# Rotating a matrix on one core: loads and stores in turn on two DMA queues instead of one queue for each direction

## The chip, the core and the metric

The kernel runs on one core of a Trainium2 chip. The core has five instruction streams: TensorE (PE), VectorE (DVE), ScalarE (ACT), GpSimd (POOL) and SyncE (SP). Data moves between the chip's main memory (HBM) and the core's on-chip memory (SBUF) by 16 DMA engines. In this kernel two streams issue DMAs: SyncE, whose DMAs appear in the profile as queue q1, and ScalarE, whose DMAs appear as queue q10. The metric is the time of one execution on the device in microseconds (us); lower is better.

## The reference

```python
def setup_inputs():
    return {
        "x": np.random.randn(8192, 8192).astype(np.float32),
        "k": 1,
    }

def reference(x: np.ndarray, k: int) -> np.ndarray:
    return np.rot90(x, k)
```

With k = 1 the matrix is turned by 90 degrees against the clock: row i of the output is column 8191 - i of the input. It is a transpose with the columns taken from the last to the first. Nothing is added or multiplied. 268 MB are read and 268 MB are written.

## The kernel before, in words

**Tiles.** The input is cut into 16 macro tiles of 1024 rows by 4096 columns (`R`, `W`; KK = 16). A macro tile kk is read by 8 loads (t = 0 to 7) of 128 full rows of the macro tile each, 2 MB per load, and written by 8 stores (j = 0 to 7) of 512 output rows by 1024 columns each, 2 MB per store. Loads are numbered m = 8 kk + t from 0 to 127, outputs n = 8 kk + j from 0 to 127. In the last macro tile two of the outputs are shaped otherwise (`END`).

**Memory.** There are five 2 MB buffers, `LAND` = 2 for loads and `OUTS` = 3 for outputs, and a `ring` that holds one macro tile less one chunk. The first loads also use the output buffers. From load 9 on the loads take the two landing buffers in turn, and output n uses the buffer that output n-3 had, up to the last macro tile. So load n+9 needs what load n+7 brought to be out of the buffer.

**Steps.** For each load m VectorE waits until it has landed, and writes it to the ring with its columns reversed (line 349). Chunks whose output goes through TensorE are only copied; the others are also transposed within 32 x 32 blocks (STREAM_TRANSPOSE). The ring places that load m takes are those that output m-8 gives free, so VectorE first waits until output m-8 has been taken from the ring. An output is made in one of two ways:

- *Moved outputs.* The 32 x 32 blocks are already turned, and have only to be put in their places. This is done by 16 copies of 32 partitions: VectorE does 1 (line 331), GpSimd 9 (line 310), ScalarE 6 (lines 410 and 419). GpSimd waits for ScalarE's share before its eighth piece and for VectorE's before its ninth, so the end of GpSimd's ninth piece says that the whole output is ready (`s_pool`).
- *TensorE outputs.* TensorE transposes 128 x 128 blocks into PSUM (line 387), and ScalarE copies them to the output buffer (line 429). These are j = 0 and 4 in most macro tiles (`BY_PE`), all j in the first and the last one, and j = 0, 2, 4, 6, 7 in the last but one.

So there are 81 moved outputs: j = 1, 2, 3, 5, 6, 7 in 13 macro tiles and j = 1, 3, 5 in one more.

**What sets the order.** Each engine runs its own list of instructions in the order in which it was written, and waits on semaphores in between: `by_gpsimd`, `by_sync`, `by_vector`, `by_tensor`, `by_scalar`. There is no scheduler. A wait ahead of a DMA therefore holds all that comes behind it in the list of the engine that issues the DMA. `taken(wait, m)` waits until load m has been reversed out of its buffer, `room_for(wait, n)` until the buffer of output n is free, `load_in_turn(e, m)` waits for the buffer's last load to be taken and issues load m.

**Queues.** The first ten loads (`EARLY`) are spread over both queues: 0, 2 and 4 on SyncE, 1, 3 and 5 on ScalarE, and 6 to 9 in halves on both (`BOTH`). From load 10 on, all loads are issued by SyncE (`by_sync`, line 313), and all 128 stores by ScalarE (line 437), each at the end of ScalarE's own work for that output: for a moved output after a wait for `s_pool`, for a TensorE output after its copies out of PSUM.

Of the kernel before, what the change touches and what calls it, by code (L numbers as in the profile page):

```python
# [6 lines left out]
P = 128  # L7
# [10 lines left out]
CH = G * P  # L18
# [6 lines left out]
BY_PE = [0, 4]  # L25
EARLY = range(T + 2)
BOTH = EARLY[-4:]

END = T // 2

# [31 lines left out]
def kernel(tc: tile.TileContext, x: bass.AP, k: bass.AP, out: bass.AP):  # L62
    nc = tc.nc
# [3 lines left out]
    N, M = x.shape  # L67
    dt = x.dtype
    macros = [(r0, c0) for r0 in range(0, N, R) for c0 in range(0, M, W)]
    KK = len(macros)  # L70
    n_out = KK * J
    n_load = KK * T
# [3 lines left out]
    outs = [(kk, range(T), [j]) for kk in range(KK - 1) for j in range(J)]  # L76
# [5 lines left out]
    outs = [(*o, [(j, g * P) for j in reversed(o[2]) for g in range(G)]) for o in outs]  # L82
# [6 lines left out]
    def in_quadrants(kk, j):  # L89
        return j not in by_pe(kk)  # L90

    moved = [in_quadrants(kk, js[0]) for kk, _, js, _ in outs]
# [3 lines left out]
    for n, (kk, ts, js, blocks) in enumerate(outs):  # L96
        if moved[n]:
            continue
        rows = len(ts) * P
# [14 lines left out]
    def moved_until(n):  # L114
        return sum(moved[: n + 1])

    def turned_until(n):
        return sum(len(parts[i]) for i in range(n + 1) if i in parts)

    with tc.tile_critical():  # L120
        head = nc.alloc_sbuf_tensor("head", [P, HEAD], dt)
        ident, scratch = head[:, :P], head[:, P : P + 1]
        bufs = [nc.alloc_sbuf_tensor(f"buf{i}", [P, F], dt) for i in range(LAND + OUTS)]
# [11 lines left out]
        s_store = [nc.alloc_semaphore(f"s_store{i}") for i in range(LAND + OUTS)]  # L135
        s_rev = nc.alloc_semaphore("s_rev")
        s_half = nc.alloc_semaphore("s_half")
        s_ev = nc.alloc_semaphore("s_ev")
# [4 lines left out]
        s_pool = nc.alloc_semaphore("s_pool")  # L143

        def load_buf(m):
            if m < T:
                return m % (LAND + OUTS)
            return LAND + 2 if m == T else (m - T - 1) % LAND

        def out_buf(n):  # L150
            e = n - (KK * J - J)
            if e < 0:
                return LAND + (n + 1) % OUTS
            ends = [load_buf(n_load - 2)]
            ends += [LAND + (KK * J - J + i + 1) % OUTS for i in range(OUTS)]
            ends += [load_buf(n_load - 1)]
            return ends[e % len(ends)]

        def once(e):
            seen = {}  # L160

            def wait(sem, n):
                if seen.get(sem, 0) < n:
                    seen[sem] = n
                    e.wait_ge(sem, n)

            return wait

        def room_for(wait, n):
            b = out_buf(n)  # L170
            stores = [i for i in range(n) if out_buf(i) == b]
            loads = [i for i in range(n_load) if load_buf(i) == b]
            if stores:
                wait(s_store[b], 16 * len(stores))
            elif loads:
                taken(wait, loads[-1])

        def taken(wait, m):
            kk, t = divmod(m, T)
            wait(s_rev, max(rev[m, j] for j in range(J)))  # L180
            if t == T - 1 and kk < KK - 1:
                wait(s_corner, kk + 1)  # L182
# [18 lines left out]
        for m in range(n_load):  # L201
            kk, t = divmod(m, T)
# [16 lines left out]
        def at(v, first, dims):  # L219
            return bass.AP(  # L220
                tensor=v.tensor, offset=v[:, first : first + 1].offset, ap=[v.ap[0], *dims]
            )
# [11 lines left out]
        def moves(n, share):  # L234
            kk, ts, (j,), _ = outs[n]
            rows = len(ts) * P
            places = [slot(kk, t, j) for t in ts if (t, j) != (T - 1, J - 1)]
            ((step, tiles),) = strides(places, CH)
            for a, q in share:
                yield (  # L240
                    at(
                        bufs[out_buf(n)][q * Q : q * Q + Q, :],
                        a * Q,
                        [[rows, G], [P, tiles], [1, Q]],
                    ),
                    at(
                        ring[a * Q : a * Q + Q, :],
                        places[0] * CH + q * Q,
                        [[P, G], [step, tiles], [1, Q]],
                    ),  # L250
                )
# [3 lines left out]
        def load(e, m):  # L255
            r0, c0 = macros[m // T]
            b = load_buf(m)
            rows = slice(0, P)
            if m in BOTH:
                rows = slice(0 if e is nc.sync else 1, P, 2)  # L260
            r = r0 + m % T * P
            e.dma_start(  # L262
                out=bufs[b][rows, :], in_=x[r : r + P, c0 : c0 + W][rows, :]
            ).then_inc(s_land[b], 16)

        def queues(m):
            if m in BOTH:
                return [nc.sync, nc.scalar]
            return [nc.scalar if m in EARLY and m % 2 else nc.sync]

        def load_in_turn(e, m):
            if e not in queues(m):
                return
            last = [i for i in range(m) if load_buf(i) == load_buf(m)]
            taken(e.wait_ge, last[-1])
            load(e, m)

        def landings(m):
            return 16 * sum(1 + (i in BOTH) for i in range(m + 1) if load_buf(i) == load_buf(m))

# [4 lines left out]
        for m in range(LAND + OUTS):  # L285
            for e in queues(m):
                load(e, m)

        def by_gpsimd(e):
# [12 lines left out]
            for n, (kk, _, js, _) in enumerate(outs):  # L302
                if moved[n]:
# [6 lines left out]
                        i = e.tensor_copy(out=to, in_=of)  # L310
                    i.then_inc(s_pool, 1)

        def by_sync(e):
            for m in range(LAND + OUTS, n_load):
                load_in_turn(e, m)
            for b in range(LAND + OUTS):
                n = sum(out_buf(i) == b for i in range(n_out))
                if n:
                    e.wait_ge(s_store[b], 16 * n)
# [76 lines left out]
        def by_scalar(e):  # L396
            wait = once(e)
            e.wait_ge(s_id, 2)
            e.copy(scratch, ident[:, :1])  # L399
            for m in EARLY[LAND + OUTS :]:  # L400
                load_in_turn(e, m)
            for n, (kk, ts, js, blocks) in enumerate(outs):
                r0, c0 = macros[kk]
                rows = len(ts) * P
                b = out_buf(n)
                if moved[n] or (kk < KK - 1 and js[0] == J - 1):
                    room_for(wait, n)
                todo = list(moves(n, pairs[BY_DVE + BY_POOL :])) if moved[n] else []
                for to, of in todo[:1]:
                    e.copy(to, of)  # L410
                if kk < KK - 1 and js[0] == J - 1:
                    e.wait_ge(s_corner, kk + 1)
                    e.copy(  # L413
                        at(bufs[b][:], rows - P, [[rows, G], [1, P]]),
                        at(corner, 0, [[P, G], [1, P]]),
                    ).then_inc(s_freed, 1)
                if moved[n]:
                    for to, of in todo[1:]:
                        i = e.copy(to, of)  # L419
                    i.then_inc(s_act, 1)  # L420
                    e.wait_ge(s_pool, moved_until(n))
                else:
                    for k, h, cols in parts[n]:
                        e.wait_ge(s_half, k + 1)
                        run, deep = len(cols) * P, 1
                        if cols[-1] - cols[0] >= run:
                            run = P * sum(f // rows == cols[0] // rows for f in cols)
                            deep = len(cols) * P // run
                        e.copy(  # L429
                            at(bufs[b][:], cols[0], [[rows, deep], [1, run]]),  # L430
                            at(ps[h][:], 0, [[run, deep], [1, run]]),
                        ).then_inc(s_ev, 1)
                    e.wait_ge(s_ev, turned_until(n))
                groups = len(blocks)
                top = M - c0 - js[0] * CH - groups * P
                left = r0 + ts[0] * P
                e.dma_start(  # L437
                    out=out[top : top + groups * P, left : left + rows].rearrange(
                        "(g m) f -> m g f", m=P
                    ),  # L440
                    in_=bufs[b][:, : groups * rows].rearrange("m (g f) -> m g f", f=rows),
                ).then_inc(s_store[b], 16)

        by_gpsimd(nc.gpsimd)
        by_sync(nc.sync)
        by_vector(nc.vector)
        by_tensor(nc.tensor)
        by_scalar(nc.scalar)


# [33 lines left out]
```

## Time and profile before

| | |
|---|---|
| time, median of 3 runs | 1260.06 us (1260.0 to 1260.36) |
| the profiled execution's own time | 1260.13 us |
| its span | 1258.3 us |
| busy: PE, DVE, ACT, POOL | 332.2, 616.5, 682.0, 803.8 us |
| moved by DMA | 537.22 MB, 427 GB/s over the span |
| queue q10 (ScalarE) | 278.93 MB |
| queue q1 (SyncE) | 257.96 MB |
| last load seen by VectorE | 1209.66 us |
| last store issued | 1243.46 us |

The profile is of one execution. The span is the time from its first to its last instruction. Busy time counts an engine's computing instructions, and not the issue of DMAs nor waits. Of a wait the profile names what ended it. A DMA is shown twice: as an instruction on the engine that issues it (ACTq, SPq), which is done after some hundred nanoseconds, and as bytes moved by the 16 DMA engines. "To landing" is the time from the issue to the completion of the transfer, and holds what the transfer waits in its queue.

### The profile page before, as it was taken

Reading aid. Unit: us, or ns where it says so; the run is one execution under the profiler, and the core shown is the slowest. Engines: PE = TensorE matmul, PEld = TensorE weight load, DVE = VectorE, ACT = ScalarE, POOL = GpSimd, SP = SyncE. Lnnn points to the kernel's source line nnn. Section 1 sums busy time; section 2 is a strip of 40 time slices with the busy share of each in tenths; the row PEclk is TensorE's granted clock in tenths of the full one; section 3 lists DMA queues with packets and bytes.
Section 4 is the critical chain, followed back from the end, with each engine's and each line's share of the span. In section 5 each row is a group of like instructions: output and inputs, shape, how many; then the busy total and the mean of one; then the engine's idle time right before and its main releaser. Section 6 shows DMA issues by size and latency. Waiting matters only on the chain.

```text
span 1258.3 us, 5393 instructions
## 1 busy us (share of the span) xinstructions
PE 332.2 (26%) x1556; PEld 270.3 (21%) x1556; DVE 616.5 (49%) x373; ACT 682.0 (54%) x636; POOL 803.8 (64%) x735
## 2 busy tenths in 40 slices
PE   1556122221112221232202222022220222214474
PEld 0445111211112110121201212012110121203363
DVE  2544554555555555555555555555545554453310
ACT  0334565565556655565556655566555655556454
POOL 0001886767867779676787767877678776795500
PEclk9976555655555555555555555556555565556587
DMA  9999999999999999999999999999999999999998
GB/s 399 418 432 429 429 429 429 431 429 430 428 430 430 430 429 428 431 428 431 429 429 431 428 429 429 431 429 431 428 429 429 430 430 429 429 430 429 430 423 377
DMA packets 36957, 537.22 MB, mean 427 GB/s; under 512 B 4160, under 2 KB 4160, under 8 KB 4160
## 3 DMA queue, kind: packets, MB, share of 16 engines
q10 hardware_dynamic: 19184, 278.93, 52.2%
q1 hardware_dynamic: 17744, 257.96, 48.0%
q8 instruction: 12, 0.20, 0.1%
q14 instruction: 17, 0.14, 0.0%
HBM read 268.44 MB, written 268.44 MB: 427 GB/s over the span
## 4 chain that ended last, share of the span: by engine, by line
DMA 71%; DVE 16%; POOL 5%; ACT 3%; issue 3%; PE 1%; ACTq 0%; SPq 0%; DVEq 0%
DMA buf<-in_x_dram 65%; DVE ring L349 16%; DMA out_dram<-buf 5%; POOL buf L310 5%; ACT buf L429 3%; PE ps L387 1%; ACTq L437 0%; DVE buf L331 0%; PE ps L373 0%; SPq L262 0%; DVE buf L344 0%; DVEq L336 0%; SPq L479 0%; SPq L182 0%; SPq L120 0%
## 5 line engine op out<-in xcount | busy, mean ns | idle before, releaser
L310 POOL COPY buf<-ring 32x1024 f32<-32x1024 f32 (+1 forms) x729 | 803.1, 1102 | 383.9 <-DMA out_dram<-buf 343.6
L387 PE MATMUL ps<-head,ring 128*128 128x128 f32 x1496 | 318.6, 386 | 878.7 <-DVE ring L349 431.5
L387 PEld LDWEIGHTS ps<-head,ring 128*128 128x128 f32 x1496 | 259.6, 201 | 934.9 <-DVE ring L349 440.3
L349 DVE COPY ring<-buf 128x1024 f32<-128x1024 f32 (+5 forms) x152 | 161.6, 1069 | 595.8 <-DMA buf<-in_x_dram 573.6
L419 ACT COPY buf<-ring 32x1024 f32<-32x1024 f32 (+1 forms) x405 | 414.8, 1024 | 4.9
L349 DVE STREAM_TRANSPOSE ring<-buf 128x3072 f32<-128x3072 f32 (+2 forms) x125 | 357.8, 2871 | 0.0
L429 ACT COPY buf<-ps 128x2048 f32<-128x2048 f32 (+1 forms) x133 | 174.2, 1364 | 256.7 <-PE ps L387 182.2
L410 ACT COPY buf<-ring 32x1024 f32<-32x1024 f32 x81 | 82.9, 1023 | 289.9 <-POOL buf L310 230.6
L331 DVE COPY buf<-ring 32x1024 f32<-32x1024 f32 x81 | 108.4, 1339 | 0.0
L373 PE MATMUL ps<-head,buf 128*128 128x128 f32 x60 | 16.7, 434 | 30.3 <-DVE buf L344 30.3
L373 PEld LDWEIGHTS ps<-head,buf 128*128 128x128 f32 x60 | 10.9, 218 | 35.7 <-DVE buf L344 35.7
L413 ACT COPY buf<-ps 128x512 f32<-128x512 f32 x15 | 8.8, 586 | 8.1 <-DMA out_dram<-buf 7.9
L344 DVE COPY buf<-buf 128x512 f32<-128x512 f32 x15 | 5.8, 387 | 0.0
L399 ACT ACT_TABLE_LOAD x1 | 1.3, 1283 | 1.9 <-issue 1.9
L290 POOL MEMSET head<- 128x128 f32 x1 | 0.2, 205 | 0.5 <-SPq L120 0.5
L292 POOL TENSOR_SCALAR_AFFINE_SELECT head<-head 128x128 f32<-128x128 f32 x1 | 0.3, 294 | 0.2 <-POOL head L290 0.2
L465 POOL MEMSET const-float32-0.0<- 128x1 f32 x1 | 0.1, 98 | 0.2 <-issue 0.2
L399 ACT COPY head<-head 128x1 f32<-128x1 f32 x1 | 0.2, 192 | 0.0
L465 POOL MEMSET const-bfloat16-1.0<- 128x1 bf16 x1 | 0.1, 102 | 0.0
L465 POOL MEMSET const-uint8-127<- 128x1 uint8 x1 | 0.1, 101 | 0.0
L465 POOL MEMSET const-float32-1.0<- 128x1 f32 x1 | 0.1, 98 | 0.0
## 6 DMA issues: line engine op xcount, KB each, us to landing
out_dram<-buf ACTq DMA_DIRECT2D x128, 2048.0 KB, 18.5
buf<-in_x_dram SPq DMA_DIRECT2D x121, 2048.0 KB, 15.2
buf<-in_x_dram ACTq DMA_DIRECT2D x3, 2048.0 KB, 17.3
buf<-in_x_dram SPq DMA_DIRECT2D x4, 1024.0 KB, 16.2
buf<-in_x_dram ACTq DMA_DIRECT2D x4, 1024.0 KB, 16.5
```

The source lines that it names most:

```text
L310: i = e.tensor_copy(out=to, in_=of)
L331: i = e.tensor_copy(out=to, in_=of)
L344: e.tensor_copy(out=at(bufs[b][:], 0, [[CH, 1], [1, CH]]), in_=landed(b, js)).then_inc(s_rev, 1)
L349: turn(out=chunk(kk, t, js), in_=landed(b, js)).then_inc(s_rev, 1)
L373: i = e.transpose(corner[:, g * P : g * P + P], bufs[load_buf(m)][:, g * P : g * P + P], ident,)
L387: i = e.transpose(ps[h][:, to : to + P], chunk(kk, t, [j])[:, 0, off : off + P], ident,)
L399: e.copy(scratch, ident[:, :1])
L410: e.copy(to, of)
L413: e.copy(at(bufs[b][:], rows - P, [[rows, G], [1, P]]), at(corner, 0, [[P, G], [1, P]]),).then_inc(s_freed, 1)
L419: i = e.copy(to, of)
L429: e.copy(at(bufs[b][:], cols[0], [[rows, deep], [1, run]]), at(ps[h][:], 0, [[run, deep], [1, run]]),).then_inc(s_ev, 1)
L465: nc = _bacc.Bacc("TRN2", target_bir_lowering=False, num_devices=1)
```

## The change

From load 10 and output 0 on, each of the two queues carries loads and stores in turn. Loads with an even number are issued by SyncE, those with an odd number by ScalarE. Stores of outputs with an odd number up to 117 are issued by SyncE, each behind the load with the number n+9; the others are issued by ScalarE as before. For an output n with an even number ScalarE also issues load n+9, before the store of n: in a TensorE output behind the copies out of PSUM, in a moved output between its third and its fourth piece (`THEN` = 3). For an output with an odd number ScalarE goes on to the next output without waiting for `s_pool`; SyncE waits in its place. The copies, the buffers, the tiles and the waits of VectorE, TensorE and GpSimd are the same.

```diff
+THEN = 3
...
         def queues(m):
             if m in BOTH:
                 return [nc.sync, nc.scalar]
-            return [nc.scalar if m in EARLY and m % 2 else nc.sync]
+            return [nc.scalar if m % 2 else nc.sync]
...
+        def store(e, n):
+            kk, ts, js, blocks = outs[n]
+            r0, c0 = macros[kk]
+            rows = len(ts) * P
+            groups = len(blocks)
+            top = M - c0 - js[0] * CH - groups * P
+            left = r0 + ts[0] * P
+            if moved[n]:
+                e.wait_ge(s_pool, moved_until(n))
+            else:
+                e.wait_ge(s_ev, turned_until(n))
+            e.dma_start(
+                out=out[top : top + groups * P, left : left + rows].rearrange(
+                    "(g m) f -> m g f", m=P
+                ),
+                in_=bufs[out_buf(n)][:, : groups * rows].rearrange("m (g f) -> m g f", f=rows),
+            ).then_inc(s_store[out_buf(n)], 16)
+
         def by_sync(e):
             for m in range(LAND + OUTS, n_load):
                 load_in_turn(e, m)
+                if m >= EARLY.stop and m % 2 == 0:
+                    store(e, m - EARLY.stop + 1)
...
             for n, (kk, ts, js, blocks) in enumerate(outs):
-                r0, c0 = macros[kk]
                 rows = len(ts) * P
                 b = out_buf(n)
+                m = n + EARLY.stop - 1
+                own = [m] if n % 2 == 0 and EARLY.stop <= m < n_load else []
...
                 if moved[n]:
-                    for to, of in todo[1:]:
+                    for c, (to, of) in enumerate(todo[1:], 1):
+                        if c == THEN:
+                            for m in own:
+                                load_in_turn(e, m)
                         i = e.copy(to, of)
                     i.then_inc(s_act, 1)
-                    e.wait_ge(s_pool, moved_until(n))
                 else:
...
-                    e.wait_ge(s_ev, turned_until(n))
-                groups = len(blocks)
...
-                e.dma_start(
...
-                ).then_inc(s_store[b], 16)
+                    for m in own:
+                        load_in_turn(e, m)
+                if n % 2 == 0 or n + EARLY.stop > n_load:
+                    store(e, n)
```

More of the change, by code (lines that the diff above doesn't have):

```diff
@@ L432, in by_scalar @@
                         ).then_inc(s_ev, 1)
-                    e.wait_ge(s_ev, turned_until(n))
-                groups = len(blocks)
[L435 to L441, printed above, removed]
-                ).then_inc(s_store[b], 16)
+                    for m in own:
+                        load_in_turn(e, m)
+                if n % 2 == 0 or n + EARLY.stop > n_load:
+                    store(e, n)
         by_gpsimd(nc.gpsimd)
```

## The prediction, made before the changed kernel was run

> **What bounds the kernel now.** I read the page first: the slices, then the queues and the DMA issues.
>
> ```profile
> DMA  9999999999999999999999999999999999999998
> GB/s 399 418 432 429 429 429 429 431 429 430 428 430 430 430 429 428 431 428 431 429 429 431 428 429 429 431 429 431 428 429 429 430 430 429 429 430 429 430 423 377
> ...
> q10 hardware_dynamic: 19184, 278.93, 52.2%
> q1 hardware_dynamic: 17744, 257.96, 48.0%
> ...
> out_dram<-buf ACTq DMA_DIRECT2D x128, 2048.0 KB, 18.5
> buf<-in_x_dram SPq DMA_DIRECT2D x121, 2048.0 KB, 15.2
> ```
>
> The 16 DMA engines are busy in every slice and move 428 to 432 GB/s in all but the first two and the last two. q10 (ScalarE's) and q1 (SyncE's) take 52.2 + 48.0 = 100.2% of the engines' span, in proportion to their bytes, so a byte costs the same on either. No compute engine is above 64%. Next the stretches of time: columns are length, busy time of PE, its weight loads, DVE, ACT and POOL, granted clock, DMA share, GB/s.
>
> ```profile
> 4.00:50.00 46.00, 12.68 (x49) 9.12 (x50) 21.01 (x12) 3.70 (x3) 0.00 (x0) 1.00 1.01 431
> 500.00:700.00 200.00, 43.09 (x175) 34.29 (x175) 106.55 (x66) 113.00 (x109) 149.54 (x138) 0.52 1.01 430
> 900.00:1100.00 200.00, 44.89 (x189) 36.43 (x190) 102.09 (x66) 115.09 (x111) 150.70 (x137) 0.54 1.01 429
> 1218.00:1226.00 8.00, 6.96 (x60) 6.45 (x61) 0.00 (x0) 6.85 (x4) 0.00 (x0) 1.00 0.99 416
> 1226.00:1252.00 26.00, 13.64 (x119) 12.53 (x116) 0.00 (x0) 14.95 (x9) 0.00 (x0) 0.88 1.01 426
> 1252.00:1258.30 6.30, 0.00 (x0) 0.00 (x0) 0.00 (x0) 0.00 (x0) 0.00 (x0) 0.50 0.43 182
> ```
>
> Loads nearly alone (4 to 50 us, both queues) run at 431, loads beside stores at 429 to 430, stores alone on one queue (1226 to 1252) at 426. So one queue by itself nearly fills the engines, and no mix of directions is much better than another. The page's 537.22 MB at 429.3 GB/s, the mean of the middle, take 1251.4 us. The other 6.9 us of the 1258.3 us span are the start (33 and 319 GB/s in the first two 2 us steps: 1.85 + 0.51 us), one dip (270 in the step 50 to 52: 0.74), the 416 row (0.25) and the end (6.3 x (1 - 182/429.3) = 3.63), together 6.98. Last, the chain of waits, for the slack between the engines.
>
> ```profile
> DVE ring L349 <- DMA buf<-in_x_dram: 573.6, 120, 13.0
> ...
> POOL buf L310 <- DMA out_dram<-buf: 343.6, 29, 120.9
> ...
> DVE ring L349 <- POOL buf L310: 19.1, 4, 5.3
> ```
>
> VectorE waits for loads 120 times and for GpSimd four times; GpSimd's waits are for stores that must give back a buffer. Both are consumers of the DMA, not its brake.
>
> **The change part by part.**
>
> *Count of issues.* SyncE issued 7 + 118 = 125 DMAs, all loads; now 66 loads and 59 stores, 125. ScalarE issued 7 loads and 128 stores, 135; now 66 loads and 69 stores, 135. An issue holds ScalarE for 0.55 us and SyncE for 0.33 us before (the tile's rows), so no engine gains issue time. Bytes and shapes are equal. Cost: 0.
>
> *What SyncE's new wait holds up.* For odd n it waits for output n and issues its store, then load n+11. That load needs tile n+9 reversed, and VectorE waits for output n+1 before it does that. So a store on SyncE never holds a load that could have gone: 0.
>
> *What ScalarE's new wait holds up.* For even n it issues load n+9, which needs tile n+7 reversed. For a moved n this stands between its third and fourth piece; GpSimd's eighth piece waits for ScalarE's last. Output 2 of one row of outputs, before:
>
> ```profile
> 599.13 21.90 POOL L310 COPY buf<-ring 32x1024 f32<-32x1024 f32 x19 [0.61 <-DVE buf L331]
> 600.19 0.55 ACTq L437 DMA_DIRECT2D out_dram<-buf  x1
> 600.78 1.04 ACT L410 COPY buf<-ring 32x1024 f32<-32x1024 f32 x1 [4.33 <-POOL buf L310]
> 601.83 5.25 ACT L419 COPY buf<-ring 32x1024 f32<-32x1024 f32 x5
> 602.85 1.11 DVE L349 COPY ring<-buf 128x1024 f32<-128x1024 f32 x1 [3.79 <-DMA buf<-in_x_dram]
> 603.88 3.36 DVE L349 STREAM_TRANSPOSE ring<-buf 128x3072 f32<-128x3072 f32 x1
> 607.27 9.69 SPq L262 DMA_DIRECT2D buf<-in_x_dram  x2
> 610.62 0.55 ACTq L437 DMA_DIRECT2D out_dram<-buf  x1
> ```
>
> ScalarE's three first pieces would be done at 603.9, the tile is reversed at 607.24, the load goes at 607.3, and the other three pieces end at 607.85 + 3.15 = 611.0 instead of 607.1. GpSimd, whose nine pieces ran from 600.19 to 610.62, reaches its eighth at 600.19 + 7/9 x 10.43 = 608.3 and would stand 2.7 us. In these old phases output 2 is ready at 613.3, and VectorE, whose load landed at 612.62, starts 0.7 us later. There are 26 such outputs (j = 2 and 6 of 13 macro tiles).
>
> *What the order within a queue does.* Each queue now serves load, store, load, store, each 2 MB taking 9.76 us while the other queue is busy (4.194 MB at 429.7 GB/s). I follow one row of outputs by hand: A is the moment ScalarE's queue has moved tile 1; a landing is seen about 1 us after the last byte (an estimate from the first load: two loads at 431 GB/s from 2.36 us on end at 12.1, VectorE starts at 13.02); a moved output takes 10.43 us of GpSimd (600.19 to 610.62) from when its buffer is free; a tile is reversed in 4.4 us. Output 1 gets its buffer at A-8.8 and is ready at A+1.7; tile 1 is reversed at A+6.1, so the load behind it is issued 3.7 us before its queue reaches it (A+9.76). Output 2 starts at A+1.7; ScalarE's last pieces end at A+9.8, when GpSimd reaches its eighth, so it no longer stands; ready A+12.1, tile 2 reversed A+16.5, needed A+19.5. Output 3: ready A+22.6, tile 3 reversed A+27.0, needed A+29.3. Output 4 goes through TensorE and is early. The same steps for tiles 4 to 8 leave 4.6, 3.7, 3.1, 1.6 and 4.2 us. Before, a load was issued some 4 us before its predecessor ended (607.27 against a landing at 612.62). So the slack shrinks, to 1.6 us at worst, and every load is still in time; stores have 6 us and more. If a load is late, its queue is dry while the other still holds a whole transfer, and the 426 row says that one queue carries on at nearly full rate; the engines stop only when a load is late by its slack plus the 4.9 us of that transfer: 6.5 us at the worst place. Cost between 0 and the 26 x 0.7 = 18 us of VectorE's delay in the old phases; I take 0, being nearest to the rows where the DMA engines stay at 429 GB/s though VectorE idles 573.6 us.
>
> *Start and end.* Queue order changes after the first store (47.31 us), so start and dip stay. At the end the last load lands at 1209.66 us and the stores left over empty one queue, before and after. Load 127 stands ahead of store 118 instead of beside it, which can only fill the 416 row: at most -0.25 us, taken as 0.
>
> Sum: 1258.3 + 0; the profiled execution took 1260.13 us, 1.83 beyond its span, and the median is 1260.06. Forecast 1260.1.
>
> **The rivals.**
>
> *Slower: the extra waits stretch a row of outputs.* Place: ScalarE's load between pieces, and GpSimd behind it, at j = 2 and 6. GpSimd idles 7.6 and 8.6 us per row of outputs (621.03 to 628.62, then 659.0 to 667.6) for store buffers. A store now stands behind a load in its queue, so its buffer returns later, by up to about the 3.5 us that a landing of 18.5 us grows to 22; twice that plus 2 x 2.7 us of waits is 12.4 of the 16.2 us. It decides from there on, when delays pass the 6.5 us above. Then each run of three moved outputs loses 1.4 us (from A+6.1 to A+27.0 between tiles 1 and 3 reversed, 20.9 us against 2 x 9.76): 13 x 2 x 1.4 = 36 us, 1296; half of it absorbed at the TensorE outputs, 1278; a fifth left, 1267. For: the 1.6 us. Against: 573.6 us of VectorE waiting for loads.
> The Trainium skill (Perfetto Trace Analysis, section DMA Optimizations) advises the opposite of the change: one issuing engine for inputs and another for outputs, "to allow more dynamic spread". By that rule this rival happens and 1267 to 1296 would be the time; the trace of before, which has the separated form, cannot show the mixed one.
>
> *Faster: the mixed rate rises to that of loads alone.* If packets of one direction follow one another, the stretch 52 to 1218 could run at 431 instead of 429.3: 1166 x (1 - 429.3/431) = 4.6 us, 1255.5. For: the 431 row. Against: the stores must then run in one direction too, and theirs is 426; the average is 428.5.
>
> *Slower: turning round costs the engines.* Some 236 changes of direction inside queues are new. The nearest row is the dip when a first store joins, 0.74 us; the other queue covers nearly all of it. At 5% uncovered, 236 x 0.037 = 9 us, 1269. At all of it, 175 us, which the steady 428 to 431 with both directions side by side speaks against.
>
> **How the numbers follow.** A measurement of this kernel tells about 0.2% (2.5 us) from no change. No change: 0.62. Loads' rate or some other gain: 0.15. Stretched rows: 0.16, of which half above 1268. Turning: 0.07, half above 1268. So faster 0.15, same 0.62, slower 0.23. The range from 1255 (the faster rival with half a microsecond to spare) to 1268 leaves out about 0.04 below and 0.12 above; the likeliest case alone is 1259 to 1262.
>
> **What would show it.** Right: both queues near 267 MB and 50%, slices at 428 to 431 from the third on, SyncE's queue waiting for GpSimd and ScalarE without that wait, GpSimd waiting for ScalarE at its eighth piece, VectorE waiting for GpSimd more than 19.1 us, loads still the main thing it waits for. Wrong by the slower rivals: slices under 425 with a DMA share under 1.00 (stretch) or at 1.00 (turning). Wrong by the faster one: slices at 431 to 432 with the same share.

## The result, and the profile after

The changed kernel takes 1263.57 us (median of 22 runs, 1260.36 to 1270.95) against 1260.16 us (22 runs, 1259.96 to 1260.57). The ratio is 1.0026, with a 95% interval of 1.0018 to 1.0034: slower by about 0.26%. What the median doesn't tell is the scatter. Before, all runs lie within 0.6 us; after, one run is as fast as before and one is 10.8 us slower. The profiled execution took 1261.39 us with a span of 1259.6 us, so it shows only 1.3 us of the loss. Lines of the page after:

```profile
DMA  9999999999999999999999999999999999999998
GB/s 398 422 425 429 430 427 430 429 430 430 428 430 429 431 429 429 429 430 429 429 430 430 428 430 429 430 429 430 429 430 430 430 428 429 428 428 430 426 422 370
...
q10 hardware_dynamic: 19184, 278.93, 52.0%
q1 hardware_dynamic: 17744, 257.96, 48.1%
...
out_dram<-buf ACTq DMA_DIRECT2D x69, 2048.0 KB, 19.5
buf<-in_x_dram ACTq DMA_DIRECT2D x62, 2048.0 KB, 13.8
buf<-in_x_dram SPq DMA_DIRECT2D x62, 2048.0 KB, 14.6
out_dram<-buf SPq DMA_DIRECT2D x59, 2048.0 KB, 18.0
```

The last four lines show that the change does what it says: each queue has loads and stores. From the third slice (425 against 432) on the rate is nearly what it was. The stretches after (columns as before: length, busy time of PE, its weight loads, DVE, ACT, POOL, granted clock, DMA share, GB/s):

```profile
4.00:50.00 46.00, 12.60 (x48) 9.03 (x49) 20.98 (x12) 3.70 (x3) 0.00 (x0) 1.00 1.01 430
500.00:700.00 200.00, 37.30 (x168) 30.04 (x169) 105.85 (x66) 115.44 (x111) 150.04 (x139) 0.53 1.01 429
900.00:1100.00 200.00, 44.89 (x192) 37.41 (x190) 104.19 (x65) 113.78 (x110) 149.26 (x136) 0.54 1.01 429
1200.00:1218.00 18.00, 15.95 (x116) 14.57 (x115) 3.58 (x4) 13.06 (x9) 0.00 (x0) 0.85 1.00 421
1218.00:1226.00 8.00, 6.96 (x61) 6.42 (x60) 0.00 (x0) 6.76 (x5) 0.00 (x0) 1.00 1.02 426
1252.00:1259.60 7.60, 0.00 (x0) 0.00 (x0) 0.00 (x0) 0.00 (x0) 0.00 (x0) 0.50 0.46 196
```

Before, the stretch 1200 to 1218 was:

```profile
1200.00:1218.00 18.00, 11.13 (x77) 10.18 (x75) 4.88 (x4) 7.74 (x5) 0.00 (x0) 0.81 1.01 427
```

The middle still runs at 429. The stretch 1200 to 1218 has fallen from 427 to 421 and the end is longer; 1218 to 1226 has risen from 416 to 426. The chain of waits has changed much more than the time:

```profile
POOL buf L311 <- DMA out_dram<-buf: 350.5, 29, 122.4
DVE ring L370 <- DMA buf<-in_x_dram: 299.1, 67, 13.1
DVE ring L370 <- POOL buf L311: 290.1, 57, 8.5
...
ACT buf L444 <- DVE ring L370: 87.4, 26, 4.9
...
POOL buf L311 <- ACT buf L444: 7.4, 24, 1.3
```

VectorE used to wait for a load nearly always (573.6 us), and for GpSimd 19.1 us. Now it waits for GpSimd 290.1 us, almost as long as for loads. So loads land earlier than they are wanted, and outputs are ready later; the kernel has less in hand. One run of three moved outputs in the timeline after (start, length, engine, line, and in brackets the idle time before and what ended it) shows how:

```profile
514.67 18.27 POOL L311 COPY buf<-ring 32x1024 f32<-32x1024 f32 x16 [9.93 <-DMA out_dram<-buf]
...
524.69 0.54 SPq L325 DMA_DIRECT2D out_dram<-buf  x1
524.76 1.54 DVE L370 COPY ring<-buf 128x1024 f32<-128x1024 f32 x1 [6.37 <-POOL buf L311]
...
529.62 0.34 ACTq L263 DMA_DIRECT2D buf<-in_x_dram  x1
530.00 3.15 ACT L444 COPY buf<-ring 32x1024 f32<-32x1024 f32 x3 [3.73 <-DVE ring L370]
533.21 12.52 POOL L311 COPY buf<-ring 32x1024 f32<-32x1024 f32 x11 [0.27 <-ACT buf L444]
535.34 0.57 ACTq L325 DMA_DIRECT2D out_dram<-buf  x1
535.41 1.54 DVE L370 COPY ring<-buf 128x1024 f32<-128x1024 f32 x1 [4.45 <-POOL buf L311]
...
545.76 0.55 SPq L325 DMA_DIRECT2D out_dram<-buf  x1
545.83 0.69 DVE L370 COPY ring<-buf 128x1024 f32<-128x1024 f32 x1 [4.22 <-POOL buf L311]
```

GpSimd gets its buffer at 514.67; in the old kernel the same output began at 511.50:

```profile
511.50 8.93 POOL L310 COPY buf<-ring 32x1024 f32<-32x1024 f32 x8 [8.63 <-DMA out_dram<-buf]
```

From there outputs 1, 2 and 3 are ready at 524.69, 535.34 and 545.76, 10.4 to 10.7 us apart, and each time it is GpSimd that VectorE waits for. ScalarE's wait of 3.73 us costs GpSimd 0.27 us.

**Where the time went in the traces.** The trace has every packet of both queues and 16 completion marks of every transfer. As there are 16 DMA engines, I read the marks as one from each. I summed the bytes that the two queues had moved by a given moment after the first packet, took the difference to the kernel before, and divided by 429.3 GB/s: so many us behind. Beside it stands how far apart the 16 marks of the last store to land lie, and how much later than before the last packet ended. The last two columns are about loads 12 to 127, 116 loads. *Lead* is the time from the issue of a load to the last mark of the transfer ahead of it in its queue: how early the load is. The value given is the one below which a tenth of the loads lie. *First done* counts the loads that were issued when the first mark of the transfer ahead had already come, so that one engine at least had nothing left to do in that queue. The runs below "changed, 2nd" are those of the next section.

```text
                      us behind at              16 marks of   last packet         first
run            200   600  1050  1100  1200 us   last store    later by     lead   done
before           0     0     0     0     0        3.1 us         0          4.9     0
changed        0.2   0.2   0.2   0.4   0.6        4.0            1.3        2.4    85
changed, 2nd   0.0   0.0   0.1   0.1   0.8        5.9            2.8        2.4    51
wait only     -0.1   0.0   0.0   0.0   0.0        3.3            0.0        4.7     4
load later    -0.1   0.9   0.9   1.0   1.8        3.8            2.7        2.8    89
swapped        0.0   3.4   4.9   4.9   5.5        2.0            5.6        1.5    41
late only      0.0  -0.1   0.0  -0.1   0.2        6.5            3.0        4.9     9
early, abrupt  0.5   1.1   1.2   4.4   4.3        1.8            4.9        2.5    91
early, smooth  0.2   0.2   0.6   0.6   1.3        2.6            1.2        2.5    48
store first   12.9  43.2  83.9  87.5  99.1        1.9          103.9       -7.8    80
piece moved   -0.1  -0.2  -0.2  -0.2  -0.1        4.2            0.3        4.0    19
its control   -0.1   0.0   0.0  -0.1   0.0        3.9            0.8        4.9     0
both repairs   0.0   0.0   0.0   0.0   0.0        4.3            0.4        4.0     9
```

Two kinds of loss can be told apart. *Dry moments*: bytes that fall behind in steps, by 1200 us 0.6 and 0.8 us in the two traced executions of the changed kernel, in the second nearly all of it behind 1100 us. And an *uneven finish*: the marks of the last store lie 4 to 6 us apart instead of 3, and the last one sets the time. The last stores don't make this unevenness. It is there when the last load lands (its marks lie 3.8 us apart before, 3.6 and 5.9 in the changed kernel, 6.2 in late only), and it changes little from there to the end.

### The profile page after: what moved, and what is told of

The parts are those of the page before. It is cut to its first block, busy times and chain, and to the rows that moved or that the text cites. A ratio compares the mean times of both kernels' runs of the same rounds, so it can differ in the third digit from the quotient of the medians.

```text
span 1259.6 us, 5393 instructions
## 1 busy us (share of the span) xinstructions
PE 312.7 (25%) x1556; PEld 259.3 (21%) x1556; DVE 618.9 (49%) x373; ACT 683.4 (54%) x636; POOL 803.2 (64%) x735
## 3 DMA queue, kind: packets, MB, share of 16 engines
q10 hardware_dynamic: 19184, 278.93, 52.0%
q1 hardware_dynamic: 17744, 257.96, 48.1%
## 4 chain that ended last, share of the span: by engine, by line
DMA 45%; POOL 28%; DVE 14%; ACT 9%; issue 2%; ACTq 1%; PE 1%; SPq 0%; DVEq 0%
POOL buf L311 28%; DMA out_dram<-buf 25%; DMA buf<-in_x_dram 20%; DVE ring L370 14%; ACT buf L444 6%; ACT buf L453 3%; ACTq L263 1%; PE ps L408 1%; ACTq L325 0%; PE ps L394 0%; SPq L263 0%; DVEq L357 0%; DVE buf L365 0%; SPq L497 0%; SPq L121 0%
## 5 line engine op out<-in xcount | busy, mean ns | idle before, releaser
L408 PE MATMUL ps<-head,ring 128*128 128x128 f32 x1496 | 299.1, 371 | 895.0 <-DVE ring L370 434.4
L370 DVE COPY ring<-buf 128x1024 f32<-128x1024 f32 (+5 forms) x152 | 169.4, 1121 | 592.4 <-DMA buf<-in_x_dram 299.1
L408 PEld LDWEIGHTS ps<-head,ring 128*128 128x128 f32 x1496 | 248.6, 194 | 942.7 <-DVE ring L370 441.4
L352 DVE COPY buf<-ring 32x1024 f32<-32x1024 f32 x81 | 102.9, 1270 | 0.0
## 6 DMA issues: line engine op xcount, KB each, us to landing
out_dram<-buf ACTq DMA_DIRECT2D x69, 2048.0 KB, 19.5
```

What stands on the lines that cost most here:

```text
L370: turn(out=chunk(kk, t, js), in_=landed(b, js)).then_inc(s_rev, 1)
L408: i = e.transpose(ps[h][:, to : to + P], chunk(kk, t, [j])[:, 0, off : off + P], ident,)
```

## The experiments

Each is compared with the kernel before, run on the same chip. Two theories stood at first: *the waits* (ScalarE's new wait delays GpSimd, VectorE and the loads) and *the queues* (transfers stand behind one another). In the diffs, the lines are against the changed kernel unless it says otherwise.

### The changed kernel again

> The changed kernel once more, for a second trace beside the one of 1261.39 us. Its times so far went from 1260.4 to 1271.0 us with a median of 1263.6, against 1260.0 to 1260.6 before. Both theories (the waits: ScalarE's new waits delay GpSimd, VectorE and the loads; the queues: loads and stores stand behind one another) expect a median of 1262 to 1265 us and a spread of several us. If the trace is of a longer execution it shows in which slices the DMA engines lose time: slices below 425 GB/s in the middle speak for stretched rows of outputs, only the first and last slices for start and end.

1262.96 us (9 runs, 1260.35 to 1266.43), ratio 1.0023 [1.0014, 1.0033]. The result and the scatter repeat. The trace is of an execution of 1262.96 us, and its middle is again at 427 to 431; the loss is in the last 100 us or so:

```profile
GB/s 399 420 429 429 430 429 429 430 430 429 429 430 430 430 428 430 429 429 430 429 429 431 428 427 430 431 428 429 430 428 430 430 427 430 430 429 428 424 421 349
```

### ScalarE's wait alone

Against the kernel before:

```diff
-                    for to, of in todo[1:]:
+                    for c, (to, of) in enumerate(todo[1:], 1):
+                        if c == 3 and n % 2 == 0:
+                            taken(e.wait_ge, n + T - 1)
                         i = e.copy(to, of)
```

> The kernel before with one wait added: for even moved n ScalarE waits between its third and fourth piece until load n+7 is reversed, as the changed kernel does, but issues no load there; all loads stay on SyncE, all stores on ScalarE. The waits: 1262 to 1265 us with a spread of several us, and VectorE waits for GpSimd some 290 us as in the changed kernel. The queues: 1260.0 to 1260.6 us, no spread, VectorE's wait for GpSimd well under 150 us.

1260.14 us (11 runs, 1259.92 to 1260.42), ratio 1.0001 [0.9992, 1.0009]. Its waits:

```profile
DVE ring L349 <- DMA buf<-in_x_dram: 470.4, 95, 13.2
...
DVE ring L349 <- POOL buf L310: 122.6, 29, 5.3
...
POOL buf L310 <- ACT buf L421: 36.0, 25, 2.4
```

The wait is there: GpSimd stands 36.0 us for it and VectorE 122.6 us for GpSimd. It costs nothing: with the old queues the loads keep their lead (4.7 against 4.9 us). The theory of the waits falls as a theory by itself.

### The load behind ScalarE's sixth piece

```diff
                     for c, (to, of) in enumerate(todo[1:], 1):
-                        if c == THEN:
-                            for m in own:
-                                load_in_turn(e, m)
                         i = e.copy(to, of)
                     i.then_inc(s_act, 1)
+                    for m in own:
+                        load_in_turn(e, m)
```

> The changed kernel with ScalarE's own load behind its sixth piece instead of its third, so that GpSimd no longer waits for it; the queues still carry loads and stores in turn. The waits: back to 1260 to 1261 us, VectorE's wait for GpSimd back towards 19 us. The queues: 1262 to 1265 us with the spread, landings still uneven.

1265.47 us (6 runs, 1262.4 to 1268.72), ratio 1.0043 [1.0029, 1.0057]: no faster than the changed kernel, and by the medians some 2 us slower, though GpSimd waits for ScalarE no more. The two intervals overlap, so the 2 us are not certain. Neither theory had said that it would be slower. What the edit does besides is to issue the load later, which suggests that lateness of loads counts. The trace lies 0.9 us behind already at 600 us.

### The directions apart, on the other engines

```diff
-            return [nc.scalar if m % 2 else nc.sync]
+            return [nc.scalar if m % 2 or m > EARLY.stop else nc.sync]
...
-                if m >= EARLY.stop and m % 2 == 0:
-                    store(e, m - EARLY.stop + 1)
+            for n in range(n_out):
+                store(e, n)
...
-                own = [m] if n % 2 == 0 and EARLY.stop <= m < n_load else []
+                own = [m] if EARLY.stop < m < n_load else []
...
-                if n % 2 == 0 or n + EARLY.stop > n_load:
-                    store(e, n)
```

> The directions apart again, but on the other engines: loads 11 to 127 on ScalarE, each between its third and fourth piece (or behind the copies out of PSUM), all stores and load 10 on SyncE. ScalarE now waits at all 81 moved outputs instead of 26, and no queue mixes directions after the start. The waits: 1265 us or more. The queues: 1260 to 1261 us without spread.

1264.02 us (6 runs, 1262.12 to 1266.54), ratio 1.0033 [1.0022, 1.0044]. Neither forecast had this time. No queue mixes directions here, and it is about as slow and scattered as the changed kernel. So mixing is not needed for a loss of this size; loads issued out of ScalarE's list of work are enough. It need not be the same loss: GpSimd now stands for ScalarE 166.7 us instead of 7.4, and the dry moments are spread over the whole run:

```profile
GB/s 398 420 430 428 430 429 429 431 424 427 429 419 428 425 430 420 416 430 430 431 429 427 430 429 430 427 430 427 423 431 424 427 428 428 429 422 430 429 421 377
...
POOL buf L311 <- ACT buf L444: 166.7, 78, 5.8
```

### Mixed queues in the first 13 macro tiles only, and in the last three only

The cut is at output 104. For the first kernel the condition `n < CUT` is added to the changed kernel's four places, for the second `n >= CUT`:

```diff
+CUT = 104
...
-            return [nc.scalar if m % 2 else nc.sync]
+            n = m - EARLY.stop + 1
+            return [nc.scalar if m % 2 and (m in EARLY or n < CUT) else nc.sync]
...
-                if m >= EARLY.stop and m % 2 == 0:
+                n = m - EARLY.stop + 1
+                if m >= EARLY.stop and m % 2 == 0 and n < CUT:
...
-                own = [m] if n % 2 == 0 and EARLY.stop <= m < n_load else []
+                own = [m] if n % 2 == 0 and EARLY.stop <= m < n_load and n < CUT else []
...
-                if n % 2 == 0 or n + EARLY.stop > n_load:
+                if n % 2 == 0 or n + EARLY.stop > n_load or not (n < CUT):
```

> Loads and stores in turn only up to output 103 (13 of 16 macro tiles); from output 104 on all loads on SyncE and all stores on ScalarE again. Theory of the last tiles (a store stands behind its queue's load, the buffer comes back later, GpSimd starts a moved output later, VectorE waits for it and the next load is issued too late, and only in the last but one macro tile, where a moved output takes GpSimd 12 instead of 10.4 us, is there no slack left): 1260.0 to 1260.8 us, little spread, GB/s from 1100 to 1218 us back at 428 to 429. Rival (the mixed order loses time anywhere, at random): 1262 to 1264 us with a spread of several us.

> The complement: the old queues up to output 103, loads and stores in turn from output 104 on. Theory of the last tiles: all of the loss, 1262 to 1264 us with the spread, GB/s of 421 to 427 between 1150 and 1218 us. Rival: 3/16 of the loss, 1260.1 to 1260.9 us.

Early only: 1261.97 us (12 runs, 1260.07 to 1268.28), ratio 1.0022 [1.001, 1.0034]. Late only: 1262.45 us (11 runs, 1261.25 to 1263.9), ratio 1.0019 [1.001, 1.0027]. The early kernel's trace has a dip that belongs to neither theory, but to the cut:

```profile
1060.00:1080.00 20.00, 3.46 (x15) 3.06 (x15) 6.05 (x6) 11.73 (x12) 15.81 (x14) 0.50 1.01 429
1080.00:1100.00 20.00, 4.15 (x17) 3.35 (x17) 10.41 (x10) 10.43 (x10) 15.48 (x15) 0.59 1.00 370
```

At the cut load 113 stood on SyncE's queue behind load 112 *and* store 103. So the experiment was repeated with the return made smooth (lines against the early kernel):

```diff
-                if m >= EARLY.stop and m % 2 == 0 and n < CUT:
+                if m >= EARLY.stop and m % 2 == 0 and n < CUT - 2:
...
-                if n % 2 == 0 or n + EARLY.stop > n_load or not (n < CUT):
+                if n % 2 == 0 or n + EARLY.stop > n_load or n >= CUT - 2:
```

> As the run that mixed only up to output 103, but with a smooth return to the old queues: store 103 goes to ScalarE, so that load 113 on SyncE follows load 112 directly and does not stand behind load 112 and a store. Its dip around 1070 to 1110 us (398 and 394 GB/s, 2.6 us) should go in any case. If the rest of the loss sits in the last three macro tiles: 1260.0 to 1260.6 us. If the mixed order also loses time at random in the middle: a median of 1260.3 to 1261.5 us with single runs of several us more.

1261.34 us (11 runs, 1260.01 to 1266.34), ratio 1.0011 [1.0002, 1.002]. The dip has shrunk from 3.2 us to 0.7 (0.6 us behind at 1100 us, 1.3 at 1200; no slice between the third and the 38th below 421), and what is left is the forecast of a loss at random: a median 1.2 us up and one run of several us. The first 13 macro tiles thus cost 1.15 us at the median (1261.34 - 1260.19), the rest of the dip among it, and the last three 2.40 us (1262.45 - 1260.05); together 3.55, close to the change's loss of 3.4. The theory that all of it sits in the last tiles falls; by the medians two thirds of it do, in a part that holds 3/16 of the work. The intervals of the two ratios leave 0.3 to 2.5 us for the one and 1.3 to 3.4 us for the other. In these traces, one of each kernel, the uneven finish appears where the last tiles are mixed (6.5 us in late only) and not where they are not (1.8 and 2.6 us).

### ScalarE's store ahead of its load

```diff
-                    for m in own:
-                        load_in_turn(e, m)
                 if n % 2 == 0 or n + EARLY.stop > n_load:
                     store(e, n)
+                if not moved[n]:
+                    for m in own:
+                        load_in_turn(e, m)
```

> The changed kernel with ScalarE's store ahead of its own load in the TensorE outputs (in the moved ones as before between the third and fourth piece). The store then stands ahead of that load in the queue and gives its buffer back earlier, while the load is issued at most 1 to 2 us later. Theory of the last tiles: the stores on which GpSimd waits in the last but one macro tile land earlier, so 1260.3 to 1261.5 us; VectorE's wait for GpSimd falls. Rival (loads that are issued late by ScalarE are the cause, and not the stores): same as or slower than the changed kernel, 1263 to 1266 us.

1362.17 us (5 runs, 1359.96 to 1364.61), ratio 1.0811 [1.0797, 1.0824]: 100 us slower, which nobody expected. At the outputs made by TensorE, ScalarE's two DMAs change places in one queue; they go out within 5 us of each other in both kernels, and the load goes as soon as its buffer is free in both. The trace of this kernel:

```profile
504.64 0.55 ACTq L325 DMA_DIRECT2D out_dram<-buf  x1
...
509.35 0.33 ACTq L263 DMA_DIRECT2D buf<-in_x_dram  x1
...
529.13 0.69 DVE L370 COPY ring<-buf 128x1024 f32<-128x1024 f32 x1 [14.59 <-DMA buf<-in_x_dram]
...
533.52 3.15 ACT L444 COPY buf<-ring 32x1024 f32<-32x1024 f32 x3 [14.32 <-DVE ring L370]
...
536.73 4.42 POOL L311 COPY buf<-ring 32x1024 f32<-32x1024 f32 x4 [11.00 <-ACT buf L444]
```

The load issued at 509.35 is seen at 529.13, 19.8 us later. In the changed kernel the load at the same place is issued at 549.85 and seen at 563.37, 13.5 us:

```profile
549.85 0.34 ACTq L263 DMA_DIRECT2D buf<-in_x_dram  x1
...
563.37 1.05 DVE L370 COPY ring<-buf 128x1024 f32<-128x1024 f32 x1 [4.71 <-DMA buf<-in_x_dram]
```

With the store first, VectorE waits 14.59 us for it, ScalarE then waits 14.32 us for VectorE before it issues the *next* load, and GpSimd 11.00 us for ScalarE. Here the waits of ScalarE do what the theory of the waits had feared, and nothing is in hand to cover them: 66 of the 116 loads are issued after the whole transfer ahead of them has landed, in the changed kernel none. Between 532 and 536 us the DMA engines are busy only 47% of the time:

```profile
532.00:536.00 4.00, 0.00 (x0) 0.00 (x0) 1.68 (x2) 2.46 (x3) 0.00 (x0) 0.50 0.47 143
```

### One piece from GpSimd to VectorE

By now the theory was one of *lost slack*: a store stands behind its queue's load, its buffer comes back later, GpSimd's 10.43 us per output then decide instead of the loads' 9.76 us, and some loads are issued too late. Then shortening GpSimd's share must help, with the queues left as they are.

```diff
-BY_DVE = 1
-BY_POOL = 9
+BY_DVE = 2
+BY_POOL = 8
```

> The changed kernel with one of GpSimd's nine pieces given to VectorE (BY_DVE 2, BY_POOL 8; the queues untouched): a moved output takes GpSimd about 9.3 instead of 10.4 us, less than the 9.76 us in which a load lands. Theory of the lost slack (a store's buffer comes back later, GpSimd's chain is then as long as the loads' period, VectorE waits for it and loads are issued late): VectorE's wait for GpSimd falls from 290 us to under 100, and the time to 1260.0 to 1261.2 us with less spread. Rival (the order of transfers within a queue costs time by itself, however early the loads are issued): 1262 to 1265 us as the changed kernel.

1260.65 us (11 runs, 1260.45 to 1263.39), ratio 1.0006 [0.9997, 1.0015]. Most of the loss and nearly all of the scatter are gone (ten of the 11 runs lie within 1.2 us), the loads' lead has risen from 2.4 to 4.0 us, and VectorE's wait for GpSimd has fallen as expected:

```profile
DVE ring L370 <- DMA buf<-in_x_dram: 383.0, 94, 13.1
...
DVE ring L370 <- POOL buf L311: 82.8, 30, 4.2
```

The same edit in the kernel before is the control:

> The kernel before with one of GpSimd's nine pieces given to VectorE (BY_DVE 2, BY_POOL 8), the control for the same edit in the changed kernel. Theory of the lost slack: the old queues had the slack anyway, so 1260.0 to 1260.4 us, the same as the kernel before within its spread. Rival (the edit is worth something by itself, with any queues, and its 2.3 us in the changed kernel say nothing of the queues): 1257 to 1259 us.

1260.97 us (11 runs, 1260.87 to 1261.18), ratio 1.0007 [0.9998, 1.0016]. It gains nothing, and even gives away 0.9 us against 1260.1. Its bytes are never behind; the last packet is 0.8 us later and the last store's 16 marks lie 3.9 us apart instead of 3.1. So with this share of the work mixed queues (1260.65) are as good as separate ones (1260.97). Both repairs together, the piece moved and the old queues from output 104 on:

> Both repairs: the piece given to VectorE, and the old queues from output 104 on. Theory of the lost slack: both sources of loss are gone, 1259.7 to 1260.4 us, spread under 1 us, as the kernel before; the mixed queues leave no gain behind even where they cost nothing. Rival (the mixed queues hold a gain of their own, hidden so far under their losses): under 1259 us.

1260.62 us (11 runs, 1260.52 to 1262.06), ratio 1.0006 [0.9997, 1.0014]. That is a little above the forecast, as the control is, and far from the rival's 1259: mixed queues hide no gain.

## Why the prediction was right, and where it was wrong

The forecast was 1260.1 us, no change; measured are 1263.6 us. That is inside the range of 1255 to 1268, thanks to the room left for the rivals and not to a term of the sum. It lies beyond the 1259 to 1262 of the likeliest case, and of the 0.2% that was to count as no change the interval of the ratio (1.0018 to 1.0034) reaches both sides. So the likeliest case did not come, if barely, and a slower one did, which had 0.23, at less than the price of either slower rival (1267 and 1269 at the least that was named).

*Right: the bound.* The rate in the middle is 429 to 430 GB/s with either order, and neither a gain from loads in a row (1255.5) nor a price for turning round (1269) shows. The rival of a higher rate and that of turning fall: in the trace a 16 KB packet of a load takes 611 ns and one of a store 615 ns, on whichever queue, before and after.

*Right: the two costs at nothing of the waits.* SyncE's wait holds no load up: each of the 63 loads that it issues from its list still had to wait for VectorE behind it.

```profile
SPq L263 <- DVE ring L370: 807.5, 63, 17.4
```

ScalarE's wait alone measures 1260.14 us, and with the new queues it costs GpSimd 7.4 us in all.

*Right in mechanism, wrong in size: the order within a queue.* The hand-worked row said that VectorE would wait for GpSimd at outputs 1, 2 and 3, that GpSimd would hardly stand for ScalarE, and that tiles 1 and 3 would be reversed 20.9 us apart. The trace has all three waits, 0.27 us, and 20.2 us (529.58 to 549.81). A slack like its 1.6 us is there too, though at another tile: in most rows the tightest load is issued 2.4 us before the last mark of the transfer ahead, 1.4 us if the 1 us is taken off that the prediction puts between the last byte and the landing. And one queue does carry on: in the trace of late only SyncE's queue, at the change of order, by its packets moved next to nothing from 1062 to 1071 us, and ScalarE's alone kept the engines full, at 432 GB/s.

The step that failed is what I concluded from this: that 1.6 us of slack, with 4.9 us more from the other queue, keeps the engines busy, cost 0. The term is 3.4 us at the median. Two things were left out. The row was one row: in the changed kernel's trace loads 20, 21, 116 and 117 are issued only 1.2 to 1.6 us before that last mark. And the slack was reckoned for a queue as a whole, while the 16 engines finish a transfer some us apart (a median of 3.1 us between 600 and 1050 us before, 4.6 after). So 85 of 116 loads (51 in the second trace) are issued when the first engine has finished the transfer ahead; before it is none, and with the piece moved 19. No run shows what one such moment costs. That the loss hangs on the lead which GpSimd leaves to the loads is shown by the moved piece: it brings back most of the lead (4.0 of 4.9 us) and, but for 0.5 us, the time, and its control doesn't gain.

*The last tiles* are less clear. In the last but one macro tile a moved output takes GpSimd 11.98 us, not 10.43 (that row was in the trace before), and its buffer comes 2.2 us later; before and after:

```profile
1137.67 11.98 POOL L310 COPY buf<-ring 32x1024 f32<-32x1024 f32 x9 [6.93 <-DMA out_dram<-buf]
...
1139.88 11.96 POOL L311 COPY buf<-ring 32x1024 f32<-32x1024 f32 x9 [8.22 <-DMA out_dram<-buf]
```

But that this costs the 2.40 us of the last three macro tiles isn't shown. Loads 122 to 127, behind these outputs, are still 5.4 us or more ahead, and in the trace of late only the bytes are 0.2 us behind at 1200 us while the last packet is 3.0 us later: most of the loss there is uneven finish. *Start and end*, taken as 0, was thus wrong at the end: the 416 row was filled, as the prediction had said, but the stretch before it fell to 421 and the last one is 1.3 us longer.

*The rival of stretched rows* came true in kind, lost slack, at about a tenth of its price of 36 us, and by the medians mostly in the last tiles and not at j = 2 and 6. Stores land after 19.5 us on ScalarE's queue and 18.0 on SyncE's, against 18.5 before and the 22 that it reckoned with. The Trainium skill (Perfetto Trace Analysis, section DMA Optimizations) says that separate engines for inputs and outputs may make sense; the runs agree in sign, by 0.26%, and not because of the directions: with the directions apart but the loads on ScalarE the kernel is as slow (1264.02), and with a piece taken from GpSimd mixing costs nothing (1260.65 against 1260.97).

*Wrong without consequence: the queues' bytes.* I expected 267 MB on each. The page has 278.93 and 257.96 MB, exactly as before, and that followed from my own count of 135 and 125 issues.

*Open.* Why the engines finish further apart when the last tiles are mixed isn't settled; the marks say only that it comes about before the last load has landed. It is no general mark of mixed queues, since the control with separate queues has some of it too (3.9 us). And the slowest executions, of the changed kernel, of 1266 to 1271 us, were never the ones traced.

## What to carry to other kernels

When the DMA engines are full in every slice, as here, don't expect a reordering of transfers to gain anything there, and read its cost from who waits for whom: here VectorE's wait for GpSimd went from 19 to 290 us while the time moved by 0.26%, and the scatter between runs rose from 0.6 to 10.6 us. Work out slack for the tightest transfer and not for the typical one, and for the DMA engine that is ahead and not for the queue as a whole: a margin of one or two us is less than the engines lay apart here. If loads and stores share a queue, try the load ahead of the store first; here that order was worth 100 us.

## What the runs showed of the hardware

- The order of two transfers in one queue matters: behind the store that it used to precede, a load was seen 19.8 instead of 13.5 us after its issue, and the kernel took 100 us longer. The Trainium skill says that transfers run on the same 16 engines and interleave, whichever engine started them (DMA: Bandwidth & Descriptors, section Issuing engines are not separate DMA queues), and that each engine takes the descriptors of one ring in their order (the same page, section Queues, rings and completion order). The steady 429 to 430 GB/s agree with the first, and this experiment with the second.
- The 16 completion marks of a transfer, read as one from each DMA engine, don't come together. Those of the last store lie 3.1 us apart in the kernel before and up to 6.5 us in these runs, a difference as large as the whole effect under study; earlier in the kernel before single transfers reach 6.3 us.
- One queue can fill the engines by itself: 432 GB/s over 9 us in which the other moved next to nothing.
